# A mixture-of-experts gate matrix: indirect accumulating DMAs into a cleared DRAM buffer, and expert selection head by head

## The chip, the cores and the metric

The kernel runs on one core of a Trainium2 chip. The metric is device time in microseconds (us) from the first to the last instruction of one execution; lower is better. All data are float32 unless a line says otherwise.

## The reference

Two layers of a decoder trunk over 512 tokens and 1024 channels. Each layer has a mixer (a gated linear recurrence, a state-space branch, a merge) and then a layer of 16384 single-neuron experts. The change touches only the expert layer, which computes for each block of 128 tokens:

```python
q = (hb @ wq).reshape(128, 8, 2, 128)                 # 8 heads, two halves
s = einsum('thpd,hpnd->thpn', q, keys)                # 128 scores per half
s1_v, s1_i = top_k(s[:, :, 0, :], 16); s2_v, s2_i = top_k(s[:, :, 1, :], 16)
cand_v = s1_v[..., :, None] + s2_v[..., None, :]      # pairs; the index is 128 * s1_i + s2_i
top_v, top_j = top_k(cand_v.reshape(128, 8, 256), 16)
gate = softmax(top_v, axis=-1)                        # 16 experts per head and token: 128 slots a token
act = gelu(einsum('thkd,td->thk', u_tab[idx], hb))
out = einsum('thk,thkd->td', gate * act, v_tab[idx])
```

A token thus uses 128 slots (8 heads of 16), and two heads may pick the same expert.

## The kernel before

The kernel is written in a tile framework that places instructions on the engine queues by their order in the program and by when their inputs are due; each queue then runs in order. TensorE is PE, VectorE DVE, ScalarE ACT, GpSimd POOL, SyncE SP.

The mixer (lines up to 787) takes its weights through `load_split`: SP loads a 128x1024 tile `raw`, ACT makes its rounded part `whi`, DVE the rest `wlo`, and each product is three matmuls (lines 131 to 133). Its head loop is at line 717.

The expert layer (`peer`) has a query and U stage and a V stage. It does not gather for most tokens. Tokens 0 to 383 (`TD` = 384, three blocks) are computed densely: A = gelu(U h) for all 16384 experts in 128 tiles of 128 (`dense_U`, stored to DRAM buffer `sA`), and then in the V stage, for each of 128 tiles, A is loaded back, multiplied by a tile W of the gate matrix (`gated`, line 1020, from DRAM buffer `sW`), split, and multiplied with the tile of V (`vmm`). W[expert, token] is the sum of the gates of the slots that chose this expert, and zero elsewhere. Tokens 384 to 511 (the last block) are done by 128 gathers of rows of U and 128 of V, one slot at a time for all 128 tokens (`gather_steps`): an indirect DMA issued by POOL into one of three buffers `gr`, then one DVE instruction of 1024 elements (`dot` at line 967, `gacc` at line 978).

The query and U stage runs as follows, each layer:
- `scores` for 16 half-heads: PE product, key product, and on DVE the top 16 for four token blocks (tiles `sv`, `sx`, lines 826 to 830).
- `select(3)` for the last block, then for blocks 0, 1, 2 `select(tb)`, each over all eight heads: candidate sums, top 16 (`tv`, `tj`), 128 instructions that look the index up (`jk`, line 875), softmax.
- `build`, 32 times per block, 96 times per layer: for four tokens, DVE makes two one-hot tiles in float16 (`P`, `Qo`) and two scaled ones (`Q`), PE forms eight products of 128x128x128 (lines 932, 933), ACT copies the 128x512 result to a staging tile `stg` (line 934). Every 24 builds, ACT issues four DMAs that write 96 tokens of `stg` to `sW` (line 938), in pieces of 384 bytes.
- After every second build one `dense_U` (`more(1)`) and one gather step (`gsteps(1)`) are written in the program: 48 of them; the other 80 follow.

The V stage needs all of `sW` for its first tile, because every tile holds all 384 tokens. 128 further gather steps are written between its tiles. The last value product waits for `gacc`.

Of the kernel before, what the change touches and what calls it, by code (L numbers as in the profile page):

```python
# [17 lines left out]
J = 8  # L18
NB = 4
# [10 lines left out]
SG = 96  # L30
# [4 lines left out]
GATE = 2.0 ** 14  # L35
# [5 lines left out]
def trunk(tc, a, dbg=None, layers=L, n_i2=128):  # L41
# [37 lines left out]
    io4 = cst.tile([128, 128, 4], F16, name="io4")  # L79
    V.tensor_copy(io4, it[:, :, None].to_broadcast([128, 128, 4]))  # L80
# [402 lines left out]
    def mixer(l, h):  # L483
# [232 lines left out]
        tb_ = tables(0)  # L716
        for e in range(J):
# [100 lines left out]
    def peer(l, h, rows, gp):  # L818
# [27 lines left out]
        def select(tb):  # L846
            val = sv[:, tb].rearrange("p (h s) k -> p h s k", s=2)
            idf = rp.tile([128, 16, 16], F32, tag="idf", name=nm("idf"), bufs=1)
            V.tensor_copy(idf, sx[:, tb])
            idv = idf[:].rearrange("p (h s) k -> p h s k", s=2)  # L850
            V.tensor_scalar(idv[:, :, 0, :], idv[:, :, 0, :], 128.0, None, op0=OP.mult)
            cv = rp.tile([128, 8, NCAND], F32, tag="cv", name=nm("cv"), bufs=1)
            ci = rp.tile([128, 8, NCAND], F32, tag="ci", name=nm("ci"), bufs=1)
            for src, dst in ((val, cv), (idv, ci)):
                for r in range(5):
                    n = CAND[r]
                    V.tensor_tensor(dst[:, :, COFF[r]:COFF[r] + n], src[:, :, 0, r:r + 1].to_broadcast([128, 8, n]),
                                    src[:, :, 1, 0:n], op=OP.add)
                V.tensor_tensor(dst[:, :, COFF[5]:COFF[8]].rearrange("p h (r b) -> p h r b", b=2),
                                src[:, :, 0, 5:8, None].to_broadcast([128, 8, 3, 2]),  # L860
                                src[:, :, 1, None, 0:2].to_broadcast([128, 8, 3, 2]), op=OP.add)
                V.tensor_tensor(dst[:, :, COFF[8]:], src[:, :, 0, 8:16],
                                src[:, :, 1, 0:1].to_broadcast([128, 8, 8]), op=OP.add)
            tv = rp.tile([128, 8, 16], F32, tag="tv", name=nm("tv"), bufs=1)
            tj = rp.tile([128, 8, 16], U32, tag="tj", name=nm("tj"), bufs=1)
            for hh in range(8):
                wk = rp.tile([128, NCAND], F32, tag="wk2", name=nm("wk2"))
                top16(tv[:, hh], tj[:, hh], cv[:, hh], wk)
            tf = rp.tile([128, 8, 16], F32, tag="tf", name=nm("tf"), bufs=1)
            V.tensor_copy(tf, tj)  # L870
            code = rp.tile([128, 8, 16], F32, tag="code", name=nm("code"), bufs=1)
            for hh in range(8):
                for k in range(16):
                    jk = rp.tile([128, NCAND], F32, tag="jk", name=nm("jk"))
                    V.scalar_tensor_tensor(jk, iof[:, 0:NCAND], tf[:, hh, k:k + 1], ci[:, hh], op0=OP.is_equal,  # L875
                                           op1=OP.mult, accum_out=code[:, hh, k:k + 1])
            cint = rp.tile([128, 128], I32, tag="cint", name=nm("cint"), bufs=1)
            V.tensor_copy(cint, code[:].rearrange("p h k -> p (h k)"))
            ii = rp.tile([128, 2, 128], I32, tag="ii", name=nm("ii"), bufs=1)
            V.tensor_scalar(ii[:, 0], cint, 7, None, op0=OP.logical_shift_right)  # L880
            V.tensor_scalar(ii[:, 1], cint, 127, None, op0=OP.bitwise_and)
            fx = rp.tile([128, 3, 128], F32, tag="fx", name=nm("fx"), bufs=1)
            V.tensor_copy(fx[:, 0:2], ii)

            gv = fx[:, 2].rearrange("p (h k) -> p h k", h=8)
            V.tensor_tensor(gv, tv, tv[:, :, 0:1].to_broadcast([128, 8, 16]), op=OP.subtract)
            S.activation(fx[:, 2], fx[:, 2], AF.Exp)
            zs = rp.tile([128, 8], F32, tag="zs", name=nm("zs"), bufs=1)
            V.tensor_reduce(zs, gv, axis=mybir.AxisListType.X, op=OP.add)
            V.reciprocal(zs, zs)  # L890
            V.scalar_tensor_tensor(gv, gv, GATE, zs[:, :, None].to_broadcast([128, 8, 16]), op0=OP.mult, op1=OP.mult)
            if tb == NB - 1:
                return fx
            pt = ptile([128, 3, 128], "pc")
            for i in range(3):
                TE.transpose(pt[:, i], fx[:, i], ident)
            st = rp.tile([128, 2, 128], F16, tag="slot", name=nm("slot"))
            S.activation(st, pt[:, 0:2], AF.Copy)
            gh = rp.tile([128, 2, 128], F16, tag="gh", name=nm("gh"))
            V.tensor_copy(gh[:, 0], pt[:, 2])  # L900
            V.tensor_tensor(gh[:, 1], pt[:, 2], gh[:, 0], op=OP.subtract)
            return st, gh

        stg = {}

        def build(tb, sel, g8):
            st, gh = sel
            NT = 4
            c = slice(NT * g8, NT * g8 + NT)
            t0 = 128 * tb + NT * g8  # L910
            n, o = divmod(t0, SG)
            if o == 0:
                stg[0] = rp.tile([128, 128, SG], F32, tag="stg", name=nm("stg"), bufs=1)
            sh = [128, 128, NT]

            def row(t):
                return t[:, None, :].to_broadcast(sh)

            P_ = rp.tile(sh, F16, tag="P", name=nm("P"))
            V.tensor_tensor(P_, io4, row(st[:, 0, c]), op=OP.is_equal)  # L920
            Q_ = rp.tile(sh, F16, tag="Qo", name=nm("Qo"))
            V.tensor_tensor(Q_, io4, row(st[:, 1, c]), op=OP.is_equal)
            Qs = []
            for i in range(2):
                q = rp.tile(sh, F16, tag=f"Q{i}", name=nm("Q"))
                V.tensor_tensor(q, Q_, row(gh[:, i, c]), op=OP.mult)
                Qs.append(q)
            for b in range(NT // 4):
                ps = ptile([128, 4, 128], "pa")
                for k in range(4):  # L930
                    t = 4 * b + k
                    TE.matmul(ps[:, k], P_[:, :, t], Qs[0][:, :, t], start=True, stop=False)  # L932
                    TE.matmul(ps[:, k], P_[:, :, t], Qs[1][:, :, t], start=False, stop=True)  # L933
                S.activation(stg[0][:, :, o + 4 * b:o + 4 * b + 4], ps[:].rearrange("p t i -> p i t"), AF.Copy,  # L934
                             scale=1.0 / GATE)
            if o + NT == SG:
                for q in range(0, 128, 32):
                    nc.scalar.dma_start(sW[l][q:q + 32, :, SG * n:SG * n + SG].rearrange("i p t -> p i t"),  # L938
                                        stg[0][:, q:q + 32])


        def gather_ids(fx):
            ids = []
            for k in range(2):
                f = gp.tile([128, 128], F32, name=nm("idx"))
                V.scalar_tensor_tensor(f, fx[:, k], 128.0, fx[:, 1 - k], op0=OP.mult, op1=OP.add)
                V.tensor_scalar(f, f, float(l * 16384), None, op0=OP.add)
                i = gp.tile([128, 128], I32, name=nm("idi"))
                V.tensor_copy(i, f)
                ids.append(i)  # L950
            gate = gp.tile([128, 128], F32, name=nm("gate"))
            V.tensor_scalar(gate, fx[:, 2], 1.0 / GATE, None, op0=OP.mult)
            return ids, gate
# [7 lines left out]
        def gather_steps(fx):  # L961
            (iu, iv), gate = gather_ids(fx)
            dot = gp.tile([128, 128], F32, name=nm("dot"))
            acc_ = gacc
            for s_ in range(128):
                g = gather(a["ur"], iu, s_)
                V.scalar_tensor_tensor(g, g, 1.0, rows, op0=OP.mult, op1=OP.mult, accum_out=dot[:, s_:s_ + 1])  # L967
                if s_ % 32 == 31:
                    b = slice(s_ - 31, s_ + 1)
                    S.activation(dot[:, b], dot[:, b], AF.Gelu_apprx_tanh)  # L970
                    V.tensor_tensor(gate[:, b], gate[:, b], dot[:, b], op=OP.mult)
                yield
            for s_ in range(128):
                g = gather(a["v"].rearrange("l i p d -> (l i p) d"), iv, s_)
                if s_ == 0:
                    V.tensor_scalar(acc_, g, gate[:, 0:1], None, op0=OP.mult)
                else:
                    V.scalar_tensor_tensor(acc_, g, gate[:, s_:s_ + 1], acc_, op0=OP.mult, op1=OP.add)  # L978
# [236 lines left out]
```

## Time and profile before

| | us |
|---|---|
| median of three runs | 4114.59 |
| lowest and highest | 4113.51, 4121.61 |
| the profiled execution, whole time | 4119.27 |
| its span from first to last instruction | 4117.5 |

| engine | busy us | share of the span |
|---|---|---|
| PE | 3748.1 | 91% |
| DVE | 3272.4 | 79% |
| ACT | 1576.5 | 38% |
| POOL | 897.0 | 22% |

Busy times are sums over the whole span; the stages differ. Matmuls overlap, so the mean length of one is longer than the distance from one to the next. On POOL an indirect DMA counts as busy while it is issued, not until its data land; "to landing" is the time from issue until the data are there. The DMA share is the mean busy share of the 16 DMA engines of the core. TensorE was granted its full clock (2.4 GHz) for most of the span, 0.956 in the mean.

### The profile page before, as it was taken

What the parts mean: (1) busy time and instruction counts of PE and PEld (TensorE: products, weight loads), DVE (VectorE), ACT (ScalarE), POOL (GpSimd) and SP (SyncE); (2) the same over time, 40 slices, a digit from 0 to 9 for tenths busy, and PEclk for the clock granted to TensorE, in tenths of its full rate; (3) what the DMA queues carried; (4) which work ended last, traced back from release to release, by engine and by line L of the source; (5) the groups of instructions that cost most, each with busy time, mean ns of one, the idle gap of its engine ahead of it and who ended that gap; (6) DMA issues with size and microseconds to landing.
All of it is one profiled execution on the core that took longest, in us unless ns stands there. A gap on an engine that the chain in (4) does not pass through costs nothing.

```text
span 4117.5 us, 63112 instructions
## 1 busy us (share of the span) xinstructions
PE 3748.1 (91%) x21878; PEld 3506.5 (85%) x21878; DVE 3272.4 (79%) x9052; ACT 1576.5 (38%) x2510; POOL 897.0 (22%) x1139
## 2 busy tenths in 40 slices
PE   6999999999698856989999999999996988699998
PEld 5888878999597856889998888789996878699998
DVE  6998778999797769998757777779997976688874
ACT  3554534434233322344443445333342333233332
POOL 7443100033132235532000000000331213222210
PEclk9999999999798978999999999999998989899999
DMA  5222462498788899999843334624987788999994
GB/s 193 72 68 73 156 195 85 150 333 306 215 285 262 281 295 329 362 355 327 280 155 117 123 116 161 211 89 143 322 305 238 262 261 283 306 348 344 347 311 142
DMA packets 463889, 947.60 MB, mean 230 GB/s; under 512 B 169728, under 2 KB 288576, under 8 KB 461520
## 3 DMA queue, kind: packets, MB, share of 16 engines
q1 hardware_dynamic: 220448, 572.75, 41.0%
q0 software_dynamic: 73952, 268.56, 18.9%
q10 hardware_dynamic: 169168, 102.25, 8.4%
q8 instruction: 172, 2.82, 0.3%
q14 instruction: 149, 1.22, 0.1%
HBM read 814.44 MB, written 128.97 MB: 229 GB/s over the span
## 4 chain that ended last, share of the span: by engine, by line
PE 67%; DVE 14%; DMA 7%; ACTq 4%; issue 4%; ACT 2%; POOL 2%; SPq 0%; DVEq 0%; POOLq 0%
PE mm L131 11%; PE mm L132 11%; PE mm L133 11%; ACTq L938 3%; DVE jk L875 3%; PE mm L1037 3%; PE mm L1038 3%; PE mm L1036 3%; DVE wlo L115 3%; DMA gr<-ur,idi 2%; DMA gr<-v,idi 2%; PE pa L933 2%; PE pa L932 2%; PE pa L1037 2%; PE pb L1037 2%
## 5 line engine op out<-in xcount | busy, mean ns | idle before, releaser
L131 PE MATMUL mm<-ahi,whi 128*128 128x384 f32 (+1 forms) x3360 | 1225.2, 366 | 88.3 <-ACT uo L797 82.2
L113 ACT ACTIVATE whi<-raw 128x1024 fp32r<-128x1024 f32 x688 | 727.9, 1059 | 1350.6 <-PE mm L132 755.5
L132 PE MATMUL mm<-alo,whi 128*128 128x384 f32 (+1 forms) x3360 | 1221.6, 364 | 15.7 <-DVE alo L122 15.7
L133 PE MATMUL mm<-ahi,wlo 128*128 128x384 f32 (+1 forms) x3360 | 1221.5, 365 | 9.2 <-DVE wlo L115 9.0
L115 DVE TENSOR_TENSOR wlo<-raw,whi 128x1024 fp32r<-128x1024 f32 x688 | 840.9, 1223 | 378.8 <-ACT whi L113 377.8
L131 PEld LDWEIGHTS mm<-ahi,whi 128*128 128x128 f32 x3360 | 643.4, 192 | 141.1 <-ACT uo L797 86.0
L132 PEld LDWEIGHTS mm<-alo,whi 128*128 128x128 f32 x3360 | 642.4, 191 | 65.5 <-DVE alo L122 17.3
L133 PEld LDWEIGHTS mm<-ahi,wlo 128*128 128x128 f32 x3360 | 641.7, 191 | 62.4 <-DVE wlo L115 13.8
L957 POOL DMA_INDIRECT gr<-ur,idi x256 | 278.7, 1089 | 1498.4 <-DVE jk L875 567.4
L957 POOL DMA_INDIRECT gr<-v,idi x256 | 374.9, 1465 | 737.6 <-DVE gacc L978 645.0
L978 DVE SCALAR_TENSOR_TENSOR gacc<-gr,gate,gacc 128x1024 f32<-128x1024 f32 x254 | 324.6, 1278 | 38.1 <-DMA gr<-v,idi 38.0
L1036 PE MATMUL mm<-gh,whi 128*128 128x384 f32 x768 | 217.8, 341 | 141.4 <-ACT gh L1025 55.5
L967 DVE SCALAR_TENSOR_TENSOR gr<-gr,rows 128x1024 f32<-128x1024 f32 x256 | 311.1, 1217 | 17.6 <-DMA gr<-ur,idi 17.1
L1037 PE MATMUL mm<-gl,whi 128*128 128x384 f32 x768 | 260.8, 340 | 5.7 <-DVE gl L1027 5.3
L1036 PEld LDWEIGHTS mm<-gh,whi 128*128 128x128 f32 x768 | 141.8, 191 | 145.1 <-ACT gh L1025 97.7
L1038 PE MATMUL mm<-gh,wlo 128*128 128x384 f32 x768 | 254.2, 337 | 0.3 <-DVE wlo L115 0.3
L1025 ACT ACTIVATE gh<-A 128x384 fp32r<-128x384 f32 x256 | 132.7, 520 | 284.9 <-DVE A L1023 280.8
L932 PE MATMUL pa<-Q,P 128*128 128x128 f16 x768 | 197.3, 296 | 25.1 <-DVE P L920 15.9
L875 DVE SCALAR_TENSOR_TENSOR jk<-iof,tf,ci 128x50 f32<-128x50 f32 x1024 | 220.1, 267 | 0.0
L934 ACT ACTIVATE stg<-pa 128x512 f32<-128x512 f32 x192 | 114.2, 598 | 241.8 <-PE pa L933 239.5
L933 PE MATMUL pa<-Q,P 128*128 128x128 f16 x768 | 189.0, 296 | 0.2
L1036 PE MATMUL pb<-gh,whi 128*128 128x384 f32 x512 | 173.3, 338 | 0.0
(410 smaller groups left out, 6541.8 us busy)
## 6 DMA issues: line engine op xcount, KB each, us to landing
raw<-u SPq DMA_DIRECT2D x256, 512.0 KB, 5.1
raw<-v SPq DMA_DIRECT2D x256, 512.0 KB, 5.5
raw<-win SPq DMA_DIRECT2D x112, 512.0 KB, 3.7
ada<-ada SPq DMA_DIRECT2D x96, 512.0 KB, 4.8
sA<-uo ACTq DMA_DIRECT2D x256, 192.0 KB, 4.5
sW<-stg ACTq DMA_DIRECT2D x32, 1536.0 KB, 15.2
A<-sA SPq DMA_DIRECT2D x256, 192.0 KB, 5.2
W<-sW SPq DMA_DIRECT2D x256, 192.0 KB, 5.3
```

Source lines behind the costliest of these rows:

```text
L113: S.activation(hi, raw, AF.Copy)
L115: V.tensor_tensor(lo, raw, hi[:].bitcast(F32), op=OP.subtract)
L131: TE.matmul(ps, hi[:, w], ah, start=(j == 0), stop=False)
L132: TE.matmul(ps, hi[:, w], al, start=False, stop=False)
L133: TE.matmul(ps, lo[:, w], ah, start=False, stop=(j == J - 1))
L875: V.scalar_tensor_tensor(jk, iof[:, 0:NCAND], tf[:, hh, k:k + 1], ci[:, hh], op0=OP.is_equal, op1=OP.mult, accum_out=code[:, hh, k:k + 1])
L957: G.indirect_dma_start(out=g[:], out_offset=None, in_=tab, in_offset=bass.IndirectOffsetOnAxis(ap=ids[:, s_:s_ + 1], axis=0))
L967: V.scalar_tensor_tensor(g, g, 1.0, rows, op0=OP.mult, op1=OP.mult, accum_out=dot[:, s_:s_ + 1])
L978: V.scalar_tensor_tensor(acc_, g, gate[:, s_:s_ + 1], acc_, op0=OP.mult, op1=OP.add)
L1036: TE.matmul(ps, w[0][:, c], g[0], start=first, stop=False)
L1037: TE.matmul(ps, w[0][:, c], g[1], start=False, stop=False)
L1038: TE.matmul(ps, w[1][:, c], g[0], start=False, stop=last)
```

## The change

The one-hot products are gone: `build`, `P`, `Qo`, `Q`, `stg`, the transposes at the end of `select` and the stores at line 938. In their place:
- `clear` writes zeros from an SBUF tile to `sW`, in 192 DMAs of 128 KB per layer (128 pieces of 1 KB each), issued on SP in the head loop of the mixer, 24 ahead of each head.
- `select(hh)` now works on one head for all four blocks, directly after that head's two `scores`. It makes the index of each slot in `sW` (`idw`: expert row times 384 plus token) for the three dense blocks, and the expert indices (`idx`) for the last.
- `scatter(s_, tb)` is an indirect DMA issued by POOL that adds the gates of slot s_ of the 128 tokens of block tb, 4 bytes each, to their places in `sW`. 384 per layer. `gather_steps` issues three of them ahead of each of its first 128 gathers.
- `order` makes each scatter of a head wait for the 16 scatters of the same block of the head before it (two heads can hit the same place), and declares all others free of each other.
- The program order is now, per head: two `scores`, `select`, five times a `dense_U` and a gather step; then the other 88.

```diff
         for e in range(J):
+            for z in range(zn * e // J, zn * (e + 1) // J):   # zn = 192
+                clear(l, z)
             s5_in(e)
             head(e)
...
+    def clear(l, z):
+        flat = sW[l].rearrange("i p t -> (i p t)").rearrange("(z q f) -> z q f", q=128, f=ZF)
+        nc.sync.dma_start(flat[z], zero)
...
-        def select(tb):
+        def select(hh):
+            sh = [128, NB, 16]
+            val = sv[:, :, 2 * hh:2 * hh + 2]
...
+            for tb in range(NB):
+                wk = rp.tile([128, NCAND], F32, tag="wk2", name=nm("wk2"))
+                top16(tv[:, tb], tj[:, tb], cv[:, tb], wk)
...
+            V.scalar_tensor_tensor(vc, fi[:, 1], 128.0, fi[:, 0], op0=OP.mult, op1=OP.add)
+            b = slice(16 * hh, 16 * hh + 16)
...
+            V.scalar_tensor_tensor(wc, vc[:, 0:last], float(TD), tok[:].to_broadcast([128, last, 16]), op0=OP.mult,
+                                   op1=OP.add)
+            V.tensor_copy(idw[:, :, b], wc)
...
+            V.tensor_tensor(gate[:, :, b], gv, zs[:].to_broadcast(sh), op=OP.mult)
...
-        def build(tb, sel, g8):
...
+        def order(i, hh, tb):
+            i = getattr(i, "ins", i)
+            prev = waves.get((hh - 1, tb), [])
+            for p in prev:
+                tc.add_manual_dep(i, p.name, after, reason="adds of the head's predecessor have landed")
+            tc.declare_no_dep(i, group=f"w{l}", keep=prev, reason="rows of one head are distinct, blocks disjoint")
...
+        def scatter(s_, tb):
+            i = G.indirect_dma_start(out=wrows, out_offset=bass.IndirectOffsetOnAxis(ap=idw[:, tb, s_:s_ + 1], axis=0),
+                                     in_=gate[:, tb, s_:s_ + 1], in_offset=None, compute_op=OP.add)
+            order(i, s_ // 16, tb)
...
             for s_ in range(128):
-                g = gather(a["ur"], iu, s_)
+                for tb in range(NB - 1):
+                    scatter(s_, tb)
+                g = gather(a["ur"], idx[0], s_)
...
-        for p in range(16):
-            scores(p, first[3 + p] if p < 3 else dense(a["wq"][l, p], h))
-        steps[0] = gather_steps(select(NB - 1))
-        for tb in range(NB - 1):
-            sel = select(tb)
-            for g8 in range(32):
-                build(tb, sel, g8)
-                if g8 % 2:
-                    more(1)
-                    gsteps(1)
+        steps[0] = gather_steps()
+        for hh in range(8):
+            for p in (2 * hh, 2 * hh + 1):
+                scores(p, first[3 + p] if p < 3 else dense(a["wq"][l, p], h))
+            select(hh)
+            for _ in range(5):
+                more(1)
+                gsteps(1)
```

## Rows read from the trace of the kernel before

**Rows 1.** Windows by stage: us, busy PE, PEld, DVE, ACT, POOL; clock, DMA, GB/s.
```profile
60.00:500.00 440.00, 425.38 (x2602) 366.93 (x2600) 366.30 (x767) 219.53 (x441) 191.77 (x484) 0.99 0.28 87
658.00:1497.00 839.00, 726.59 (x4274) 688.09 (x4272) 694.59 (x2727) 283.99 (x417) 177.34 (x158) 0.93 0.77 249
2726.00:3561.00 835.00, 725.39 (x4277) 688.79 (x4276) 692.49 (x2719) 284.48 (x418) 181.02 (x156) 0.93 0.77 250
1497.00:2105.00 608.00, 538.48 (x3001) 530.65 (x3002) 519.14 (x1132) 235.58 (x352) 193.59 (x116) 0.95 0.90 323
3561.00:4094.00 533.00, 533.00 (x3076) 533.00 (x3076) 399.67 (x487) 196.44 (x254) 106.78 (x101) 1.00 0.89 313
```

**Rows 2.** Two source lines, by layer: first top-16, first value matmul (first start).
```profile
L826 DVE MAX8 sv<-s x64: 273/277/295, 658.1 to 752.6; 128x8 f32<-128x128 f32 x64
...
L826 DVE MAX8 sv<-s x64: 273/277/295, 2726.4 to 2820.9; 128x8 f32<-128x128 f32 x64
...
L1036 PE MATMUL mm<-gh,whi x375: 333/334/689, 1497.0 to 2101.8; 128*128 128x384 f32 x188
...
L1036 PE MATMUL mm<-gh,whi x384: 334/334/686, 3560.8 to 4088.0; 128*128 128x384 f32 x192
```

**Rows 3.** The chain that ended last (start, us, what): first and last such stall.
```profile
1068.37 7.01 ACTq L938
...
3537.64 14.90 DMA sW<-stg
```

**Rows 4.** Windows of tiles P and Q, layer 0: PE, PEld, DVE (ACT).
```profile
658.00:1497.00 839.00, 115.12 (x768) 80.72 (x768) 40.10 (x96) 0.93 0.77 249
...
658.00:1497.00 839.00, 115.12 (x768) 0.00 (x0) 74.53 (x192) 0.00 (x0) 0.93 0.77 249
```

**Rows 5.** Timeline of POOL and DVE, layer 1: start, us, [idle before <-releaser].
```profile
2890.41 0.95 POOL L957 DMA_INDIRECT gr<-ur,idi  x1 [363.87 <-DVE jk L875]
2891.66 0.94 POOL L957 DMA_INDIRECT gr<-ur,idi  x1 [0.30 <-issue]
...
2958.99 1.22 DVE L115 TENSOR_TENSOR wlo<-raw,whi 128x1024 fp32r<-128x1024 f32 x1
2959.16 1.87 POOL L957 DMA_INDIRECT gr<-ur,idi  x1 [1.93 <-DVE jk L875]
```

**Rows 6.** The source line of the gathers, whole span.
```profile
L957 POOLq EVENT_SEMAPHORE  x512: 17/17/357469, 463.6 to 3961.7; - x171
L957 POOL DMA_INDIRECT gr<-ur,idi x256: 935/939/1973, 822.3 to 3408.6; - x128
...
DMA to landing us min/median/max: 4.1/6.3/15.8
```

**Rows 7.** Windows of the gather tile, layer 0: DVE, POOL.
```profile
658.00:1497.00 839.00, 190.68 (x284) 177.34 (x158) 0.93 0.77 249
```

**Rows 8.** Timeline of POOL at the start: plain DMAs.
```profile
2.40 0.76 POOL L1096 DMA_DIRECT2D v_n1g<-n1g  x1
...
4.59 0.57 POOL L1115 DMA_DIRECT2D fg<-fg  x1
```

**Rows 9.** Windows of tiles sv, jk and tv, layer 0: DVE.
```profile
658.00:1497.00 839.00, 80.74 (x540) 0.93 0.77 249
...
658.00:1497.00 839.00, 110.85 (x1024) 0.93 0.77 249
...
658.00:1497.00 839.00, 32.64 (x260) 0.93 0.77 249
```

**Rows 10.** Page part 3, DMA queues: packets, MB, share of 16 engines.
```profile
q0 software_dynamic: 73952, 268.56, 18.9%
...
q10 hardware_dynamic: 169168, 102.25, 8.4%
```

**Rows 11.** Groups by line: the DVE work per second gather.
```profile
L978 DVE SCALAR_TENSOR_TENSOR gacc<-gr,gate,gacc 128x1024 f32<-128x1024 f32 x254 | 324.6, 1278 | 38.1 <-DMA gr<-v,idi 38.0
```

**Rows 12.** Timeline of the SP queue in the mixer of layer 0.
```profile
76.05 0.35 SPq L101 DMA_DIRECT2D raw<-win  x1
```

More of the change, by code (lines that the diff above doesn't have):

```diff
@@ L29 @@
 TD = 384
-SG = 96
+ZF = 256
 GB = 3
@@ L78, in trunk @@
     V.tensor_copy(iof, it)
-    io4 = cst.tile([128, 128, 4], F16, name="io4")
-    V.tensor_copy(io4, it[:, :, None].to_broadcast([128, 128, 4]))
+    toki = ctmp.tile([128, NB - 1], I32, name="toki")
+    G.iota(toki, pattern=[[128, NB - 1]], base=0, channel_multiplier=1)
+    tok = cst.tile([128, NB - 1, 1], F32, name="tok")
+    V.tensor_copy(tok[:, :, 0], toki)
+    zero = cst.tile([128, ZF], F32, name="zero")
+    G.memset(zero, 0.0)
     masks = cst.tile([128, 6, 128], U8, name="masks")
@@ L844, in scores @@
                 top16(sv[:, tb, p], sx[:, tb, p], s[:, tb], wk)
-        def select(tb):
[L847 to L850, printed above, removed]
+        gate = gp.tile([128, NB, 128], F32, name=f"gate{l}")
+        idw = one.tile([128, NB - 1, 128], I32, name=f"idw{l}")
+        idx = [gp.tile([128, 128], I32, name=f"idx{l}{k}") for k in range(2)]
+        def select(hh):
+            sh = [128, NB, 16]
+            val = sv[:, :, 2 * hh:2 * hh + 2]
+            idv = rp.tile([128, NB, 2, 16], F32, tag="idv", name=nm("idv"), bufs=1)
+            V.tensor_copy(idv, sx[:, :, 2 * hh:2 * hh + 2])
             V.tensor_scalar(idv[:, :, 0, :], idv[:, :, 0, :], 128.0, None, op0=OP.mult)
-            cv = rp.tile([128, 8, NCAND], F32, tag="cv", name=nm("cv"), bufs=1)
-            ci = rp.tile([128, 8, NCAND], F32, tag="ci", name=nm("ci"), bufs=1)
+            cv = rp.tile([128, NB, NCAND], F32, tag="cv", name=nm("cv"), bufs=1)
+            ci = rp.tile([128, NB, NCAND], F32, tag="ci", name=nm("ci"), bufs=1)
             for src, dst in ((val, cv), (idv, ci)):
@@ L862, in select @@
                 V.tensor_tensor(dst[:, :, COFF[8]:], src[:, :, 0, 8:16],
[L863 to L866, printed above, removed]
+                                src[:, :, 1, 0:1].to_broadcast([128, NB, 8]), op=OP.add)
+            tv = rp.tile(sh, F32, tag="tv", name=nm("tv"), bufs=1)
@@ L872, in select @@
-            for hh in range(8):
+            code = rp.tile(sh, F32, tag="code", name=nm("code"), bufs=1)
+            for tb in range(NB):
                 for k in range(16):
                     jk = rp.tile([128, NCAND], F32, tag="jk", name=nm("jk"))
-                    V.scalar_tensor_tensor(jk, iof[:, 0:NCAND], tf[:, hh, k:k + 1], ci[:, hh], op0=OP.is_equal,
-                                           op1=OP.mult, accum_out=code[:, hh, k:k + 1])
-            cint = rp.tile([128, 128], I32, tag="cint", name=nm("cint"), bufs=1)
@@ L889, in select @@
-            V.tensor_reduce(zs, gv, axis=mybir.AxisListType.X, op=OP.add)
-            V.reciprocal(zs, zs)
[L891 to L904, printed above, removed]
-        def build(tb, sel, g8):
[L907 to L939, printed above, removed]
@@ L942, in gather_ids @@
[L942 to L953, printed above, removed]
+            fi = rp.tile([128, 2, NB, 16], F32, tag="fi", name=nm("fi"), bufs=1)
@@ new lines, in select @@
+            V.tensor_copy(fi, ii)
+            vc = rp.tile(sh, F32, tag="vc", name=nm("vc"), bufs=1)
+            V.scalar_tensor_tensor(vc, fi[:, 1], 128.0, fi[:, 0], op0=OP.mult, op1=OP.add)
+            b = slice(16 * hh, 16 * hh + 16)
+            last = NB - 1
+            wc = rp.tile([128, last, 16], F32, tag="wc", name=nm("wc"), bufs=1)
+            V.scalar_tensor_tensor(wc, vc[:, 0:last], float(TD), tok[:].to_broadcast([128, last, 16]), op0=OP.mult,
+                                   op1=OP.add)
@@ new lines, in select @@
+            V.tensor_copy(idw[:, :, b], wc)
+            for o, f in ((idx[0], code), (idx[1], vc)):
+                t = rp.tile([128, 16], F32, tag="gx", name=nm("gx"))
+                V.tensor_scalar(t, f[:, last], float(l * 16384), None, op0=OP.add)
+                V.tensor_copy(o[:, b], t)
+            gv = rp.tile(sh, F32, tag="gv", name=nm("gv"), bufs=1)
+            V.tensor_tensor(gv, tv, tv[:, :, 0:1].to_broadcast(sh), op=OP.subtract)
+            S.activation(gv, gv, AF.Exp)
+            zs = rp.tile([128, NB, 1], F32, tag="zs", name=nm("zs"), bufs=1)
@@ new lines, in select @@
+            V.tensor_reduce(zs[:, :, 0], gv, axis=mybir.AxisListType.X, op=OP.add)
+            V.reciprocal(zs, zs)
+            V.tensor_tensor(gate[:, :, b], gv, zs[:].to_broadcast(sh), op=OP.mult)
+        wrows = sW[l].rearrange("i p (t o) -> (i p t) o", o=1)
+        waves = {}
+        after = mybir.DependencyInfo(mybir.DependencyClass.Sync, mybir.DependencyReason.DATA)
+        def order(i, hh, tb):
[4 more added lines that the diff above has]
+            tc.declare_no_dep(i, group=f"w{l}", keep=prev, reason="rows of one head are distinct, blocks disjoint")
+            tc.add_to_no_dep_group(f"w{l}", i)
+            waves.setdefault((hh, tb), []).append(i)
@@ L970, in gather_steps @@
                     S.activation(dot[:, b], dot[:, b], AF.Gelu_apprx_tanh)
-                    V.tensor_tensor(gate[:, b], gate[:, b], dot[:, b], op=OP.mult)
+                    V.tensor_tensor(ga[:, b], ga[:, b], dot[:, b], op=OP.mult)
                 yield
             for s_ in range(128):
-                g = gather(a["v"].rearrange("l i p d -> (l i p) d"), iv, s_)
+                g = gather(a["v"].rearrange("l i p d -> (l i p) d"), idx[1], s_)
                 if s_ == 0:
-                    V.tensor_scalar(acc_, g, gate[:, 0:1], None, op0=OP.mult)
+                    V.tensor_scalar(gacc, g, ga[:, 0:1], None, op0=OP.mult)
                 else:
-                    V.scalar_tensor_tensor(acc_, g, gate[:, s_:s_ + 1], acc_, op0=OP.mult, op1=OP.add)
+                    V.scalar_tensor_tensor(gacc, g, ga[:, s_:s_ + 1], gacc, op0=OP.mult, op1=OP.add)
                 yield
```

31 lines of the change are left out of this document (13 added, 18 removed).

## The prediction

> **What bounds the kernel now.** I read the windows by stage first, because busy shares over the whole span hide where the time is lost. The reader should see in [rows 1] that PE is full in the mixer (425 of 440 us) and in the last value stage (533 of 533), but not in the query and U stage: 727 of 839 us in layer 0, 725 of 835 in layer 1. So 112 and 110 us stand still just where the change works. I set the borders of that stage by two source lines [rows 2]: from the first top-16 (T, 658.1 and 2726.4) to the first value matmul (1497.0 and 3560.8), that is 838.9 and 834.4 us, mean 837. The chain of waits then says what the lost time is: issue stalls of the DMAs that store the gate matrix from ACT's queue, 7.0 us for the first, up to the landing of the last one, 14.9 us, straight ahead of the first value matmul [rows 3]. While ACT's queue is held, no `whi` is made and PE has no weights. The last value stage gives nothing back: its PE is full.
>
> **What goes.** The build's matmuls take 115 us of PE time per layer, `P` 40 us and `Q` 75 us of DVE [rows 4]; `Qo` has the count and shape of `P`, so another 40. ACT loses the evictions and all line 938 stalls. What PE then has left between T and the value stage is 727 - 115 = 612 us, and DVE 695 - 40 - 40 - 75 = 540. If nothing new came, the stage would take some 625 us. It is not the sum of the removed parts that counts, though, but who ends last next, and that is POOL.
>
> **POOL, the new end.** The value stage's first W tile needs all scatters, and three scatters are queued ahead of each of the first 128 gathers. So POOL must issue 512 indirect DMAs per layer before the value stage, where it issued 158 before, 30 of them already for the second table [rows 7].
>
> Price of a gather: 0.94 us [rows 6], and back to back the next one starts 1.25 us after the first [rows 5]. To this comes a lock: a gather that started 0.17 us into a 1024-element `wlo` took 1.87 us, that is, it waited until that instruction was nearly over [rows 5]. Most gathers take 0.94 all the same [rows 6], though such instructions fill a third of DVE's time, so I take it that only a start inside one is exposed, for some 1.09 us of the 1.22. The stage has 141 `wlo` and 128 dots of this size in about 800 us, 0.34 per us; a start at a random time loses 0.34 x 1.09² / 2 = 0.20 us. Gather pitch: 1.45 us. That POOL now issues without pauses makes this loss regular; before, releases by DVE itself mostly put the start beside the lock.
>
> Price of a scatter: not in this trace. It has the same 128 indices, and the sum needs one more read per row. Plain POOL DMAs of 256 and of 128 pieces took 0.76 and 0.57 us [rows 8], so 128 more pieces cost 0.19; I take half of it, since only one of the two sides grows, and get 1.55. Lower bound: no dearer than a plain DMA of 128 pieces, 0.57 + 0.31 + 0.20 = 1.08. Upper bound: two further rounds of pieces, 1.45 + 0.38 = 1.83. I stay close to the gather, which shares the index work.
>
> Start: the first scatter needs `select(0)`. One eighth of `sv`, `jk` and `tv` is (80.7 + 110.9 + 32.6) / 8 = 28 us of DVE [rows 9], and some 32 further small operations at the 0.13 us per record of `tv` add about 5. `wlo` takes 1.22 of each 4.3 us (612 us over 141 weight tiles), so 33 / 0.72 = 46 us after T.
>
> Waits between heads: the first scatter of a head and block waits for the landing of the 16 before it. Behind the waiting instruction stand all of POOL's queue, the gather and, through it, the dot in DVE's order. Gathers landed in 6.3 us (4.1 to 15.8) [rows 6]; four POOL issues at 1.5 have passed by then, so I take 2 us for each of seven changes of head, 14; bounds 0 and 70.
>
> Tail: from the last scatter's issue through its landing, the load of W, the product and the split to the first matmul, 13 us, an estimate; before, the same tail followed the last store [rows 3].
>
> Sum per layer: 46 + 128 x 1.45 + 384 x 1.55 + 14 + 13 = 46 + 186 + 595 + 27 = 854 us from T, against 837: +17, and twice that is +34. PE (612) and DVE (540) finish earlier and wait. With the bounds of the scatter alone the stage takes 673 or 961 us.
>
> **What else moves.** (a) The 30 second-table gathers that POOL did ahead of the value stage move into it, with 30 x 1.28 = 38 us of DVE per layer [rows 11]. Layer 1 has 133 us of DVE idle there, so nothing; layer 0 has 89 [rows 1] but in bursts. I take 10, bounds 0 and 38. (b) Selecting by head has twice as many small DVE instructions at half the size: some 15 us of DVE per layer, hidden as long as DVE's 540 lie under POOL's 854; a floor of 625 would feel them. (c) `clear`: 192 issues of 0.35 us on SP [rows 12] are 67 us of SP per layer, ahead of the head's weight loads, 8.4 us per head if they go in one run. The pieces cost between 33 ns (mean of queue q10: 8.4% of 16 x 4117.5 us over 169168 packets) and 168 ns (q0) [rows 10]: 24576 of them are 51 to 258 us of the 16 engines per layer, in a stage with a DMA share of 0.28 [rows 1]. Four `raw` buffers cover a run of 8.4 us, so I take 0.5 us per head, 8 in all; without that cover it would be 16 x 8.4 = 134. A gain is excluded: nothing leaves the mixer.
>
> Total: 4119.27 + 34 + 10 + 8 = 4171 for the profiled execution; it lies 4.7 above the median, so 4167 as a median, 52 us (1.3%) slower.
>
> **Rivals.** (A) The scatter is cheaper than the gather's price, and POOL ends early. Against it stands only my reading of the index work; for it, that 4 bytes per row move little. It decides below a pitch of 1.48: (837 - 46 - 186 - 27 - 9) / 384. At 1.30 the stage takes 758, in total 4119 - 158 + 18 = 3979; at 1.08, 673 and 3809. The floor of PE, some 625, gives 3713.
> (B) The DMA engines become the bound, slower than forecast. The stage uses 0.77 x 839 = 646 us of them [rows 1]; the stores go (65536 x 33 ns / 16 = 135) and 30 gathers (30 x 128 x 168 / 16 = 40), which leaves 471. The scatters add 49152 / 16 = 3072 packets per engine; from 117 ns each the sum passes 828 us. At 168 ns it is 987, plus 46 and 13: 1046 per layer, in total 4555. For it: each piece reads and writes back. Against it: 384-byte pieces are already cheap in q10's mean.
> (C) POOL is starved while heads are selected. If its queue keeps program order, only five steps stand in each head, and a head is 28 + 5 us of selection plus 7 x 1.22 + 5 x 1.3 = 48 us of DVE: 384 us for 40 steps, and the other 88 at 1.45 + 3 x 1.55 = 6.1 us are 537. With 27 that is 948, +111 per layer, 4119 + 222 + 18 = 4359. Against it: U matmuls were queued well ahead of builds that stand before them in the program, so order bends to readiness; scatters need no buffer and can fill POOL's pauses.
> (D) It doesn't do what it says: the scatters are not let into flight together, each waiting for the one before. At 6.3 + 1.25 us each, 384 are 2899 us per layer, and the total is beyond 8000. `order` is written against this. The Trainium skill's page "DMA: Bandwidth & Descriptors" says in "Rules for kernel authors" that transfers under 64 KB pay mostly overhead, and gives in "Anatomy of one DMA — SWDGE (gpsimd) path" about 2.0 us of fixed cost per DMA; by that figure, an estimate, serial scatters would be 768 us a layer, close to the 595 of my sum. The trace agrees on the overhead but not on its being in series: two gathers started 1.25 us apart while landings took 4.1 us and more [rows 5, 6].
>
> **How the numbers follow.** A change of 0.2%, 8 us, is about what this measurement can tell from none. Forecast (POOL ends the stage, 4110 to 4260): 0.40, of which 0.06 within 0.2%, 0.01 faster. A: 0.33. B: 0.14. C: 0.10. D: 0.03. Faster: 0.33 + 0.01 = 0.34; same 0.06; slower 0.33 + 0.14 + 0.10 + 0.03 = 0.60. The range from 3930 to 4400 leaves out the deep end of A (about 0.10), the upper half of B and D (about 0.10). The likeliest case alone has 4110 to 4260.
>
> **What would show it.** POOL's timeline between T and the value stage with pauses of about 0.3 us: the forecast; its last scatter tens of us ahead of the last U matmul: A. Scatters of 1.2 to 1.3 us mean length: my price. POOL waiting for landings in the middle of a head, and a DMA share near 1: B. POOL waiting for dots in the first 400 us: C. PE's lost time should now stand at the end of the U stage as one gap; no ACT issue stalls should be left. In the mixers, more than 10 us of PE idle per layer beyond before would show that `clear` is not hidden. The prediction is wrong above all if the scatter's issue is far from 1.25 us.

## The result, and the profile after

The changed kernel takes 4585.2 us in the median (4583.7 to 4589.9, four runs) beside 4117.3 for the kernel before (4113.5 to 4121.6): a ratio of 1.114, with a 95% interval from 1.112 to 1.116. It is 468 us slower. The forecast had been 4167 with a range up to 4400: the sign and the engine are right, the size is not.

The windows of the changed kernel, in the order layer 0's and layer 1's query and U stage, then the two value stages (columns as in [rows 1]):

```profile
680.50:1687.70 1007.20, 697.21 (x3494) 665.05 (x3492) 515.95 (x2433) 239.10 (x329) 775.84 (x490) 0.85 0.62 156
2967.00:3968.30 1001.30, 703.72 (x3494) 670.84 (x3492) 513.63 (x2402) 238.94 (x329) 769.38 (x490) 0.85 0.63 157
1687.70:2351.00 663.30, 558.65 (x3039) 545.53 (x3040) 568.44 (x1055) 241.00 (x357) 233.62 (x167) 0.93 0.94 339
3968.30:4556.00 587.70, 530.98 (x3041) 530.02 (x3042) 455.93 (x560) 197.44 (x255) 162.42 (x150) 0.95 0.94 329
```

Beside [rows 1, 2] the first window says that the stage grew from 839 to 1007 us and that POOL's 177 us [rows 7] became 776, while DVE's work fell from 695 to 516. The places where the 466 us between the two profiled spans (4117.5 and 4583.6) arise, by first top-16 (658.1 and 2726.4 before, 680.5 and 2967.1 after) and first value product (1497.0 and 3560.8; 1687.7 and 3968.3): start +22, stage of layer 0 +168, from there to layer 1's first top-16 +50, stage of layer 1 +167, from there to the end +59.

POOL in the middle of layer 0's stage, one line for each instruction (start us, length us, idle before it):

```profile
1005.45 2.10 POOL L935 DMA_INDIRECT sW<-gate,idw  x1 [0.31 <-issue]
1007.85 1.55 POOL L935 DMA_INDIRECT sW<-gate,idw  x1 [0.30 <-issue]
1009.70 1.99 POOL L935 DMA_INDIRECT sW<-gate,idw  x1 [0.30 <-issue]
1012.00 1.55 POOL L935 DMA_INDIRECT sW<-gate,idw  x1 [0.31 <-issue]
...
1025.06 1.55 POOL L935 DMA_INDIRECT sW<-gate,idw  x1 [0.30 <-issue]
1026.92 1.00 POOL L942 DMA_INDIRECT gr<-ur,idx  x1 [0.30 <-issue]
```

Every pause is the 0.30 us between two issues; nothing else is waited for. The source line of the scatter, over the whole span, and what waits for what in layer 0's stage (us in total, times, longest):

```profile
L935 POOL DMA_INDIRECT sW<-gate,idw x768: 1549/1561/3017, 740.3 to 3901.8; - x192
...
DMA to landing us min/median/max: 2.9/3.6/7.0
```

```profile
POOL sW L935 <- issue: 113.1, 371, 0.3
...
DVE gr L953 <- DMA gr<-ur,idx: 479.6, 78, 19.1
...
PE mm L136 <- DVE wlo L118: 278.9, 51, 15.5
```

So a scatter holds POOL for 1.56 us in the median where a gather took 0.94 [rows 6], and never less than 1.55. Its landing is recorded for 98 of the 768; the median of 3.6 us is theirs. In layer 0 the first starts 59.8 us after the first top-16; up to the last one at 1624.8 pass 884.5 us, which is 383 x 2.00 (mean 1.70 in this layer, and the pause) + 81 gathers x 1.44; and 62.9 us later comes the first value product. In between POOL waits for nothing longer than 0.3 us. DVE waits for the gathers, and PE for DVE.

### The profile page after: what moved, and what is told of

It reads as the page before. It is cut to its first block, busy times and chain, and to the rows that moved or that the text cites. A ratio compares the mean times of both kernels' runs of the same rounds, so it can differ in the third digit from the quotient of the medians.

```text
span 4583.6 us, 60457 instructions
## 1 busy us (share of the span) xinstructions
PE 3722.3 (81%) x20324; PEld 3484.4 (76%) x20324; DVE 3031.6 (66%) x8570; ACT 1488.3 (32%) x2336; POOL 2171.5 (47%) x1909
## 3 DMA queue, kind: packets, MB, share of 16 engines
q0 software_dynamic: 184544, 269.00, 23.7%
q14 instruction: 153, 1.25, 0.1%
## 5 line engine op out<-in xcount | busy, mean ns | idle before, releaser
L136 PE MATMUL mm<-ahi,wlo 128*128 128x384 f32 (+1 forms) x3360 | 1283.4, 382 | 544.7 <-DVE wlo L118 544.7
L935 POOL DMA_INDIRECT sW<-gate,idw x768 | 1294.4, 1685 | 234.1 <-issue 225.2
L134 PE MATMUL mm<-ahi,whi 128*128 128x384 f32 (+1 forms) x3360 | 1263.0, 377 | 27.2 <-ACT ahi L231 27.2
L135 PE MATMUL mm<-alo,whi 128*128 128x384 f32 (+1 forms) x3360 | 1261.5, 376 | 13.5 <-DVE alo L125 12.4
L136 PEld LDWEIGHTS mm<-ahi,wlo 128*128 128x128 f32 x3360 | 679.6, 202 | 629.6 <-DVE wlo L118 579.6
L134 PEld LDWEIGHTS mm<-ahi,whi 128*128 128x128 f32 x3360 | 680.2, 203 | 79.1 <-ACT ahi L231 29.8
L942 POOL DMA_INDIRECT gr<-v,idx x256 | 335.5, 1311 | 708.1 <-DVE gacc L964 621.8
L942 POOL DMA_INDIRECT gr<-ur,idx x256 | 306.4, 1197 | 745.0 <-DMA raw<-u 263.6
L1020 PE MATMUL pa<-gh,whi 128*128 128x384 f32 x512 | 174.1, 340 | 0.0
L1021 PE MATMUL pa<-gl,whi 128*128 128x384 f32 x512 | 172.6, 337 | 0.0
```

Of the source, the lines that this page charges most:

```text
L134: TE.matmul(ps, hi[:, w], ah, start=(j == 0), stop=False)
L135: TE.matmul(ps, hi[:, w], al, start=False, stop=False)
L136: TE.matmul(ps, lo[:, w], ah, start=False, stop=(j == J - 1))
L935: i = G.indirect_dma_start(out=wrows, out_offset=bass.IndirectOffsetOnAxis(ap=idw[:, tb, s_:s_ + 1], axis=0), in_=gate[:, tb, s_:s_ + 1], ...
L942: G.indirect_dma_start(out=g[:], out_offset=None, in_=tab, in_offset=bass.IndirectOffsetOnAxis(ap=ids[:, s_:s_ + 1], axis=0))
L1020: TE.matmul(ps, w[0][:, c], g[0], start=first, stop=False)
```

## Experiments

The theory after the result: POOL ends the stage, and the accumulating scatter is dearer to issue than anything in the trace of before. Rivals: its form (4-byte rows into DRAM), the DMA engines, the selection by head, the order of DVE's queue. Each time stands beside runs of the kernel before on the same chip (4116 to 4119 us, in the last case 4114).

**The sum taken out of the scatter.**

```diff
-  in_=gate[:, tb, s_:s_ + 1], in_offset=None, compute_op=OP.add)
+  in_=gate[:, tb, s_:s_ + 1], in_offset=None)
```

> The scatters write instead of adding (where two heads hit one place the later one stands; nothing else changes). Theory: the sum is what makes the issue dear. Undisturbed scatters then take the gather's 0.94 to 1.00 us instead of 1.55, their pitch with the lock falls from 2.00 to about 1.45, and each stage from 1004 to about 1004 - 384 x 0.55 = 793 us or to where another engine ends it; total 4160 to 4250. Rival: the form (128 rows of 4 bytes scattered into DRAM) is dear with or without the sum; scatters stay at 1.55 and the total within 10 us of 4585.

Measured: 4179.8 us, 1.016 times before (1.013 to 1.018). The scatter's line and both stages:

```profile
L935 POOL DMA_INDIRECT sW<-gate,idw x768: 965/973/2945, 742.4 to 3490.1; - x192
```

```profile
682.60:1478.70 796.10, 667.44 (x3495) 638.54 (x3493) 516.97 (x2433) 239.19 (x329) 567.30 (x490) 0.92 0.60 198
2757.00:3554.00 797.00, 669.59 (x3494) 641.16 (x3492) 513.92 (x2402) 238.96 (x328) 565.92 (x490) 0.92 0.60 198
```

The theory holds. A plain scatter costs nearly what a gather does, 0.97 us; the sum adds 0.59 to it. 4585 - 4180 = 405 of the 468 us are the sum's price. The DMA share of the stage is 0.60 here and 0.62 with the sum, so the engines that move the data are full in neither.

**Half the rows in each scatter.**

```diff
-  ap=idw[:, tb, s_:s_ + 1], ... in_=gate[:, tb, s_:s_ + 1]
+  ap=idw[0:64, tb, s_:s_ + 1], ... in_=gate[0:64, tb, s_:s_ + 1]
```

> Each scatter takes the slots of the first 64 tokens of its block only (the other half of the sums is missing); the count of 768 stays. Theory: the dear part is paid per row. An undisturbed scatter of 64 rows takes 0.8 to 1.1 us instead of 1.55, its pitch with the lock 1.3 to 1.6 instead of 2.0, the stages fall by 384 x 0.5 = 190 us or to where the gathers end them; total 4150 to 4300. Rival: it is paid once per DMA; the scatter stays within 0.1 us of 1.55 and the total within 30 us of 4585.

Measured: 4495.3 us.

```profile
L935 POOL DMA_INDIRECT sW<-gate,idw x768: 1387/1402/3393, 746.5 to 3817.2; - x192
```

Neither end, but far closer to the rival: 64 rows less save (1.561 - 1.402) = 0.16 us, 2.5 ns a row. If each row costs the same, all 128 are 0.32 of the 1.56 us, and 1.24 are paid once per DMA.

**No scatter at all.**

```diff
-                for tb in range(NB - 1):
-                    scatter(s_, tb)
```

> Leaves all 768 scatters out (the gate matrix stays zero); clears, selection by head, gathers and all products stay. Theory: only POOL's issue work makes the stage long. POOL then has 60 + 128 x 1.45 = 246 us of work in it, PE's 612 us of matmuls end it, and it takes 625 to 680 us in each layer; the value stages go back to about 608 and 533 us; the start keeps the 22 us of the clears. Total 4115 - 2 x (837 - 650) + 22 + some 20 = 3760 to 3820. Rival: selection by head or the dots' place in DVE's order stretch the stage by themselves; then it stays above 750 us without a single scatter and the total above 3960.

Measured: 3776.3 us (0.917; 0.915 to 0.920).

```profile
680.00:1335.00 655.00, 623.58 (x3493) 604.53 (x3492) 576.38 (x2514) 239.79 (x330) 196.81 (x160) 0.99 0.80 283
```

As the theory said. Selection by head, the clears and the gathers leave a stage of 655 us in which PE is busy for 624; value stages return to 621 and 556 us. The scatters alone thus cost 809 us, and the rest of the change would have gained 341. The same 3494 matmuls that took 624 us here took 697 in the changed kernel, where the granted clock was 0.85 in the mean: PE loses part of its speed in the pauses, but as a follower, since POOL has none.

**One block's scatters of three.**

```diff
-                for tb in range(NB - 1):
-                    scatter(s_, tb)
+                scatter(s_, 0)
```

> Scatters of the first block of tokens only, 128 per layer (the gate matrix has only that block). Theory: POOL has 60 + 128 x 2.0 + 128 x 1.45 = 500 us of work ahead of the value stage, less than PE's 612, and so the total stays within 40 us of the kernel without any scatter. Rival: the scatters cost time in proportion, through DMA traffic or because each one delays a gather and with it DVE; then a third of the difference between 4585 and the kernel without scatters shows, some 260 us.

Measured: 4020.9 us. The theory's number falls: 245 us over no scatter, close to a third of 809. The stage took 768 us with POOL busy for only 408 of them:

```profile
682.00:1450.00 768.00, 644.85 (x3496) 619.73 (x3495) 566.13 (x2506) 240.46 (x331) 408.15 (x278) 0.93 0.75 235
```

What DVE waited for there, up to 1500 us:

```profile
DVE gr L952 <- DMA gr<-ur,idx: 180.8, 60, 18.9
```

And the same in the stage of the kernel without any scatter:

```profile
DVE gr L951 <- DMA gr<-ur,idx: 49.7, 36, 3.6
```

With its pauses, 278 x 0.30 = 83 us, POOL was idle for 277 of 768 us, and it delayed PE all the same. The scatters of a head become ready together, stand on POOL's queue in runs of 14, some 28 us, and a dot waits in DVE's order for a gather behind the run, with the weight splits `wlo` behind the dot.

**That reading, with more buffers.** One block again, and the first table's gathers in eight buffers of their own.

```diff
-        def gather(tab, ids, s_):
-            g = gp.tile([128, D], F32, tag="gr", name=nm("gr"), bufs=GB)
+        def gather(tab, ids, s_, pool=gp, bufs=GB):
+            g = pool.tile([128, D], F32, tag="gr", name=nm("gr"), bufs=bufs)
...
-                g = gather(a["ur"], idx[0], s_)
+                g = gather(a["ur"], idx[0], s_, rp, 8)
```

> Scatters of the first block alone (the gate matrix has only that block), with eight buffers for the first table's gathers. With three, one block cost 112 us per stage over none, though POOL was not full: 16 scatters of a head go in a run of 30 us when its indices come, and a dot waits for the gather behind the run. Theory: eight gathers in flight cover most of such a run; the stage falls from 770 to 655 to 700 us, total 3800 to 3900. Rival: a run of 30 us is longer than what the buffers hold, or the gathers are not placed earlier; the total stays within 30 us of 4021.

Measured: 4104.7 us, slower than with three buffers and outside both expectations; the stage of layer 0 took 848 us. More gathers of both tables moved ahead of the value stage (220 instead of 150 in layer 0), in between the scatters, whose last start went from 1286.9 to 1416.9 us. So more buffers are no cure here, and this run does not confirm the reading; why the delay grew was not followed further.

**All scatters, eight buffers.** The same edit in the changed kernel.

> Gathers of the first table get eight buffers of their own instead of sharing three; nothing else changes. Theory: with three buffers 44 of the 128 gathers end up behind the last scatter and lie in the 63 us tail and the value stage. With eight they move ahead; POOL's sum stays, so the stage is 60 + 384 x 2.0 + 128 x 1.44 + some 15 = about 1030 us (now 1004), and the value stages give back their 50 and 59 us: total 4585 + 50 - 100 = 4510 to 4550. Rival: the place of the gathers is not set by buffers but by the dots' place in DVE's order; then nothing moves and the total stays within 10 us of 4585.

Measured: 4598.6 us. Stage and value stage of layer 0:

```profile
678.00:1741.00 1063.00, 680.79 (x3496) 649.34 (x3495) 569.40 (x2487) 240.91 (x330) 827.37 (x537) 0.83 0.62 171
1741.00:2367.00 626.00, 553.75 (x3100) 547.76 (x3100) 531.77 (x1139) 239.44 (x357) 187.32 (x121) 0.94 0.88 320
```

Half of the expectation came: the value stage gave back what it had lost (626 and 559 us to their ends, 624 and 557 before). But 537 instead of 490 POOL instructions now stood ahead of it, and the stage grew by 55 us. POOL's work is only moved; the 50 and 59 us behind the stage are gathers that POOL had no time for earlier.

**The first table's gathers and dots left out.**

```diff
-                g = gather(a["ur"], idx[0], s_)
-                V.scalar_tensor_tensor(g, g, 1.0, rows, ..., accum_out=dot[:, s_:s_ + 1])
+            V.memset(dot, 0.0)
```

> All 768 scatters stay; the 256 gathers of the first table and their dots are left out (that activation is zero). Theory: the dots couple the engines. They stand in DVE's order between the weight splits, their gathers stand behind scatters on POOL, and so PE is starved throughout. Without them POOL has only 60 + 384 x 2.0 = 830 us to do, PE runs ahead of it and then stands in one gap: the last U product before 700 us after the first top-16, the stage 830 to 850 us, DVE's waits for gathers gone; total 4585 - 2 x 160 - 2 x 50 = 4160 to 4280. Rival: scatters slow PE and DVE directly (the granted clock, DMA traffic); then wlo still comes late all through the stage and the last U product still stands within 30 us of its end.

Measured: 4350.9 us; stage 958 us, and PE still starved to its end, which was the rival's sign. The timeline shows why (start, length, idle before):

```profile
1209.61 1.54 POOL L935 DMA_INDIRECT sW<-gate,idw  x1 [0.30 <-issue]
1211.46 1.54 POOL L935 DMA_INDIRECT sW<-gate,idw  x1 [0.31 <-issue]
1213.31 0.99 POOL L942 DMA_INDIRECT gr<-v,idx  x1 [0.30 <-issue]
...
1217.52 1.28 DVE L963 SCALAR_TENSOR_TENSOR gacc<-gr,gate,gacc 128x1024 f32<-128x1024 f32 x1 [46.59 <-DMA gr<-v,idx]
1218.72 1.22 DVE L118 TENSOR_TENSOR wlo<-raw,whi 128x1024 fp32r<-128x1024 f32 x1
1219.01 2.38 POOL L935 DMA_INDIRECT sW<-gate,idw  x1 [0.31 <-issue]
...
1219.99 0.69 PE L136 MATMUL mm<-ahi,wlo 128*128 128x384 f32 x1 [38.41 <-DVE wlo L118]
```

The gathers of the second table moved up into the free places. As long as scatters last they come in groups of three, each behind a run of 48 scatters that takes POOL about 93 us. DVE stands for 46.6 us in front of one of them. That gather was issued at 1213.31 and its data were used 4.2 us later; for the rest of the wait it stood behind scatters. Then `wlo` is made, and PE runs again after 38.4 us. The edit had left such waits in place, so it decides nothing between the two; but these lines show the coupling at work.

**All gathers left out.** As above, and the second table's gathers and their `gacc` steps too.

> All 768 scatters stay; all 1024 gathers and their DVE steps are left out, of the second table too (the last block's part is zero). Without the first table's gathers alone, those of the second moved up into the same places of DVE's order and PE was held by them as before. Theory: it is these waits in DVE's order that spread PE's loss. Now the last U product comes 610 to 680 us after the first top-16, POOL's 60 + 384 x 1.9 = 790 us end the stage, and PE stands in one gap of over 100 us ahead of the first value product; stage 790 to 830 us. Rival: scatters hold DVE or PE back by themselves; the last U product stands within 30 us of the stage's end again.

Measured: 4028.0 us.

```profile
680.00:1300.00 620.00, 615.89 (x3496) 602.62 (x3495) 391.93 (x2207) 235.23 (x322) 475.39 (x279) 1.00 0.68 162
1300.00:1502.00 202.00, 0.00 (x0) 0.00 (x0) 4.71 (x21) 3.47 (x4) 162.56 (x106) 0.50 0.25 7
```

Now the theory is shown: the last U product starts 615 us after the first top-16, then PE does nothing for 202 us while POOL finishes its scatters, and the value stage begins 9 us after the last of them. Scatters do not hold PE or DVE by themselves, and neither do gathers, which without scatters left a stage of 655 us. Gathers that stand behind scatters, and for which DVE waits in order, do.

**Clears held to their head.** The zeros come from a tile made from the head's result.

```diff
+            zt = hp.tile([128, ZF], F32, tag="zt", name=nm("zt"), bufs=1)
+            G.tensor_scalar(zt, yap[:, e, 0:ZF], 0.0, None, op0=OP.mult)
+            for z in range(zn * e // J, zn * (e + 1) // J):
+                clear(l, z, zt)
...
```

> The clears of a head read a tile of zeros that is made from this head's result, so that they can't start before it; 192 stay in each layer's mixer. Theory: the 22 us by which the first top-16 of layer 0 came later are due to all 384 clears of both layers that ran in the first 273 us, at a DMA share of 0.75 to 0.93; held back they cost less: the first top-16 at 658 to 665, total 4560 to 4570. Rival: 384 issues and 49152 pieces cost the same wherever they stand, or more in the head loops, where SP's queue feeds PE; total 4580 to 4610.

Measured: 4551.7 us, 33.5 less than the changed kernel and a little more than expected; the first top-16 at 661.4 us. The clears and the first 100 us, first of the changed kernel, then held:

```profile
L802 SPq DMA_DIRECT2D sW<-zero x384: 319/450/1806, 20.6 to 273.3; - x192
...
0.00:100.00 100.00, 52.14 (x187) 41.59 (x188) 59.48 (x131) 29.61 (x44) 79.35 (x244) 0.83 0.93 311
```

```profile
L802 SPq DMA_DIRECT2D sW<-zt x384: 319/448/2394, 162.2 to 2759.1; - x192
...
0.00:100.00 100.00, 66.40 (x277) 54.48 (x278) 65.03 (x145) 33.52 (x49) 79.58 (x232) 0.95 0.54 199
```

Since nothing held them, all 384 clears of both layers had gone out in the first 273 us, at a DMA share of 0.93 in the first 100, beside the first weight loads.

**The stall of before, taken away otherwise.** One-hot products as before, but the DRAM buffer is ordered by row, chunk of 96 tokens, tile and token, so that a store writes one piece for each row. The value stage loads two tiles at a time.

```diff
-    sW = [drp.tile([128, 128, TD], F32, name=f"sW{l}") ...]
+    sW = [drp.tile([128, TD // SG, 128, SG], F32, name=f"sW{l}") ...]
-    nc.scalar.dma_start(sW[l][q:q + 32, :, SG * n:SG * n + SG].rearrange("i p t -> p i t"), stg[0][:, q:q + 32])
+    nc.scalar.dma_start(sW[l][:, n, q:q + 32], stg[0][:, q:q + 32])
...
```

> The kernel before, with its one-hot products, but the DRAM buffer of the gate matrix lies as chunk of 96 tokens, row, tile, token: each store then writes 12 KB in a row per partition (128 pieces instead of 4096), and the value stage loads two tiles at a time in pieces of 768 bytes (twice as many pieces there). Theory: what the change was to remove, some 110 us per layer of PE idle, comes from ACT's queue while it issues stores of 4096 pieces; with 128 pieces the issue is short, the stage falls from 837 to 727 to 750 us, and the total to 3900 to 3960. Rival: the stalls come from landing or from bytes, which stay; total within 40 us of 4118. A loss in the value stage from the finer loads would show as PE idle there, up to 2 x 20 us.

Measured: 4041.3 us, 0.982 times before (0.980 to 0.984): faster than both kernels. Stores of before, then stores and stage of this one:

```profile
L938 ACTq DMA_DIRECT2D sW<-stg x32: 377/5910/10732, 1068.0 to 3537.6; - x32
```

```profile
L939 ACTq DMA_DIRECT2D sW<-stg x32: 326/648/2326, 1068.0 to 3451.1; - x32
...
DMA to landing us min/median/max: 5.9/16.4/24.1
...
657.00:1460.50 803.50, 723.37 (x4276) 683.93 (x4275) 708.78 (x2740) 284.58 (x418) 208.12 (x171) 0.93 0.78 269
```

Less than half of the expected gain came: 75 us of some 160 to 220. The issue fell from 5.9 to 0.65 us, but the stage only from 839 to 803, so the issue stalls by which the prediction explained PE's 112 idle us were worth some 36 of them. The last U product now comes 80 us earlier (1371.7 for 1451.9); the one-hot products come last, and in layer 0 each chunk but the first waits for the landing of the one before, 49 us in all, because there is one staging tile.

**Two staging tiles.** The same with chunks of 48 tokens and `bufs=2` for `stg`.

> The kernel before with the contiguous gate buffer, now in chunks of 48 tokens with two staging tiles instead of one of 96; the value stage then loads in pieces of 384 bytes (four times as many as before). Theory: what is left of the stall is the one staging tile, whose next use waits 16 to 24 us for the landing of its stores (40 us of ACT waits near the end of each stage); with two the stage falls from 800 to 750 to 780 us, the value stages lose up to 20 us each; total 3980 to 4040. Rival: the value stage's DMA engines, busy 0.9 of the time, don't stand four times the pieces, and lose more there than is won: total above 4050.

Measured: 4056.0 us. Stage and value stage of layer 0:

```profile
657.00:1422.00 765.00, 717.41 (x4272) 680.44 (x4270) 692.79 (x2724) 285.59 (x417) 185.44 (x157) 0.96 0.79 273
1422.00:2073.00 651.00, 570.21 (x3102) 559.06 (x3103) 530.14 (x1142) 239.88 (x359) 154.92 (x116) 0.94 0.90 305
```

Both sides came: the stages fell by 38 and 33 us, and from the first value product on 35 us were lost in layer 0 and 53 in layer 1. The loads in pieces of 384 bytes are the change that the edit makes there, but 14 and 16 second-table gathers more also stand behind the stages (157 instead of 171 and 173 ahead of them); the two were not told apart.

## Why the prediction was right or wrong

**Price of a scatter: this is the step that failed.** It set 1.25 + 0.10 + 0.20 = 1.55 us as the pitch; 2.00 was measured in layer 0. The choice "close to the gather, which shares the index work" would have held for a plain scatter (1.15 + 0.30 = 1.45). What it left out is that the sum is another issue, 0.59 us dearer. The upper bound of 1.83 failed for the same reason: it was scaled by pieces, from plain DMAs [rows 8], and the price is paid per DMA. 384 x 0.45 = 173 us per layer is more than the 153 by which the sum of 854 missed the 1007; the other terms nearly cancel (start +14, tail +50, changes of head -14, and some -69 because only 81 of the 128 gathers stood between the scatters, which no term foresaw: partly luck).

**The lock** was sized a little high, and its reading holds. Of the 768 scatters, by the engine records at their starts, the 183 that began within a `wlo` or a dot took 2.07 us in the mean, the 422 that began while DVE was idle 1.56 and never over 1.62. With 0.2 to 0.4 us of the DVE instruction left, a scatter took 0.19 longer than 1.555; with 1.0 us or more left, 0.99 longer. The mean over all, 1.69, lies 0.14 above the shortest, 1.55. I had 0.20. In the timeline above the scatter at 1219.01 shows it: 2.38 beside a running `wlo`, 1.54 with DVE idle. The Trainium skill's page "SBUF — State Buffer" says in "Who interferes with whom" that a DVE instruction with two SBUF inputs contends with a GpSimd instruction that reads SBUF; these lengths agree.

**Start and head changes.** First scatter after 60 us, not 46. Changes of head: 14 us were set; POOL's rows show 3.0 us in 10 waits for landings in layer 0, none longer than the usual pause of 0.3. Landings took 3.6 us in the median where recorded, which other issues covered.

**Tail.** 13 us were set, 63 came. The 13 supposed that only a landing, a load and a split follow; without gathers it is 9. But 10 U tiles were still to do after the last scatter, because their splits stood behind dots in DVE's order; that PE and DVE "finish earlier and wait" was wrong. For the same reason "PE's lost time as one gap" did not come; it was spread over the stage, and the one gap appeared only when all gathers had gone.

**Moved gathers.** 10 us in layer 0 and none in layer 1 were set; 50 and 59 us came. I moved 30 gathers, those that POOL did ahead of the value stage for the second table. In fact it was 52 in layer 0: 158 indirect DMAs for gathers stood ahead of the value stage before [rows 7], 106 do now, and 22 of the first table's own lie behind its start. The DVE idle time that I counted on in layer 1 was no help, because there PE waits in one piece for the last `gacc`:

```profile
PE mm L1051 <- DVE gacc L964: 53.8, 1, 53.8
```

**Clears.** 8 us were set, spread over the heads; 22 came at the start, and 33.5 are to be had by holding them, 19 of these at the start. What failed is their place: it was read from the program's order. Held to their heads, they left the first top-16 only 3.3 us later than before (661.4 to 658.1), beside 4 set for layer 0. Where the other 14 us came from was not followed.

**What held.** PE's floor of 612 us (616 without gathers, 624 without scatters), no issue stalls of ACT, and POOL as the engine that sets the stage's length, though its last scatter came 63 us before the end.

**The rivals.** A fell: the scatter is not cheaper than the gather. B fell: its threshold was a price per piece, but the DMA share is 0.62 and POOL never stood waiting for a landing. C fell: between its first and its last scatter POOL never waited for DVE, since the scatters, which need no buffer, went ahead of the gathers; after the last one it did, 30 us in 19 waits in layer 0. D fell, landings overlap. On D I had cited the Trainium skill's page "DMA: Bandwidth & Descriptors", section "Anatomy of one DMA — SWDGE (gpsimd) path". The 768 us estimated from its fixed cost come close to the 766 that the scatters took per layer, but by another cause: that section puts most of the cost in the completion and calls descriptor generation small, while here completions overlapped and the issue on POOL was the whole of it. The two gathers by which the prediction checked that page move 512 KB each, so they said little of transfers under 64 KB; the scatters, of 512 bytes, landed in 2.9 us at the least.

**Without the sum's price** the change is still slower than before, 4180 to 4118: the stages are then 43 and 37 us shorter than before, and the start (+24 us) and the late gathers behind both stages take more back.

## What to carry to other kernels

An operation that no row shows is a price to be measured, and its bounds should not be scaled from another form of it: here the sum on an indirect DMA cost 0.59 us of POOL's time per DMA, and halving the rows saved only 0.16 of the 1.56. Ask of every step that waits in an in-order queue what stands behind it: a POOL that was idle for over a third of the stage still delayed PE, through gathers behind runs of scatters and weight splits behind dots. And before an expensive step is replaced, look at what makes it stall: the same products with stores of 128 pieces instead of 4096 made the kernel 1.8% faster than before.

## What was unexpected of the hardware

An accumulating indirect DMA of 128 rows of 4 bytes leaves 144 packets in its queue, (184544 - 73952) / 768, the plain one 32, (98528 - 73952) / 768, and yet the DMA share of the stage was 0.62 and 0.60:

```profile
q0 software_dynamic: 184544, 269.00, 23.7%
```

```profile
q0 software_dynamic: 98528, 269.00, 19.2%
```

The gathers have some 144 packets each as well (73952 over 512) and cost 0.94 us to issue; so it is not the count of packets alone that makes the issue dear. Why the sum costs POOL 0.59 us more stays open.
